# GELU times the second half, on one core: in-place GELU, packed products and three input buffers in place of two input and two output buffers

## The chip, the core and the metric

The kernel runs on one core of a Trainium2 chip. The time is device time in microseconds for one execution; before the change the median of three runs is 469.35 us (469.26 to 469.49). The core has a vector engine (VectorE, DVE in the profile), an activation engine (ScalarE, ACT), a synchronisation engine (SyncE, SP) and 16 DMA engines that move data between the chip's main memory (HBM) and the on-chip memory (SBUF), which has 128 partitions. DMA transfers are issued on a queue of SP or of ACT; an instruction waits for a semaphore to reach a count, and a finished transfer adds 16 to its semaphore.

## The reference

The input x is 32 x 512 x 2048 in float32. Each row of 2048 is cut in two halves, and the output row of 1024 is the GELU of the first half times the second half:

```python
x1, x2 = x[..., :1024], x[..., 1024:]
out = 0.5 * x1 * (1 + erf(x1 / sqrt(2))) * x2
```

That is 134.22 MB read and 67.11 MB written.

## The kernel before

The 16384 rows are cut into 16 tiles of 1024 rows. In a tile each of the 128 partitions holds R = 8 rows that lie one after the other in HBM, so that a load puts 64 KB in a row into each partition (4 rows, 32 KB, for the two halves of tile 0) and a store takes 32 KB in a row from each. There are two input buffers (x_bufs, 64 KB a partition each) and two output buffers (o_bufs, 32 KB a partition each); tile i uses number i % 2 of both.

The order on each engine is written out by hand, with one semaphore for each buffer and kind:

- SP issues the loads. Tile 0 comes in two halves, tile 1 whole; these three are issued ahead of the loop. In the loop, after tile i, SP waits until the products of tile i are done (line 108) and issues the load of tile i + 2 into the buffer that they have read (line 109). SP also issues the stores of the last two tiles.
- ACT takes each tile in pieces (5 and 3 rows; 2, 2 and 4 for the first and the last tile). Before the first piece it waits for ready[k] (line 79), which counts the load of this tile and the store that last used the same output buffer. It writes the GELU of the first half of each row into the output buffer (line 81). After the tile it waits for the products and issues the store (line 54), except for the last two tiles.
- DVE waits for each GELU piece and multiplies it, in the output buffer, with the second half of the rows in the input buffer (line 89).

Tile 0 is stored in two halves, so is tile 15; the others are stored by one transfer. At the end ACT, DVE and SP clear the semaphores, and SP waits for the last stores (line 118).

Of the kernel before, what the change touches and what calls it, by code (L numbers as in the profile page):

```python
# [1 line left out]

# [4 lines left out]

GELU = mybir.ActivationFunctionType.Gelu


@with_exitstack
def kernel(
    ctx: ExitStack,
    tc: tile.TileContext,
    x: bass.AP,
    out: bass.AP,
):
    nc = tc.nc
    P = nc.NUM_PARTITIONS

    x_flat = x.flatten_outer_dims()
    out_flat = out.flatten_outer_dims()
    n_rows, dim = x_flat.shape
    half = dim // 2

    R = 8
    x_t = x_flat.rearrange("(n p r) d -> n p r d", p=P, r=R)
    o_t = out_flat.rearrange("(n p r) d -> n p r d", p=P, r=R)
    n_tiles = x_t.shape[0]
    x_bufs = [nc.alloc_sbuf_tensor(f"x{k}_tile", [P, R, dim], x.dtype) for k in range(2)]  # L30
    o_bufs = [nc.alloc_sbuf_tensor(f"o{k}_tile", [P, R, half], out.dtype) for k in range(2)]

    first = [nc.alloc_semaphore(f"first{j}") for j in range(2)]
    ready = [nc.alloc_semaphore(f"ready{k}") for k in range(2)]
    gelu_done = nc.alloc_semaphore("gelu_done")
    mul_done = nc.alloc_semaphore("mul_done")
    tail_stored = nc.alloc_semaphore("tail_stored")
    n = {sem.name: 0 for sem in [*first, *ready, gelu_done, mul_done, tail_stored]}  # L40

    def counted(ins, sem, by):
        ins.then_inc(sem, by)
        n[sem.name] += by

    def load(i, rows, sem):
        ins = nc.sync.dma_start(out=x_bufs[i % 2][:, rows, :], in_=x_t[i][:, rows, :])  # L47
        counted(ins, sem, 16)
        return ins

    def store(queue, i, rows, sem):
        queue.wait_ge(mul_done, n[mul_done.name])
        counted(
            queue.dma_start(out=o_t[i][:, rows, :], in_=o_bufs[i % 2][:, rows, :]), sem, 16
        )

    for ins in (  # L60
        load(0, slice(0, 4), first[0]),
        load(0, slice(4, 8), first[1]),
        load(1, slice(0, 8), ready[1]),
    ):
        tc.no_tile_sem_insts.add(ins.ins.name)
    tc.close()
    tc.compile()  # L67

    for i in range(n_tiles):
        k = i % 2  # L70
        last = i == n_tiles - 1
        pieces = i == 0 or last
        steps = ((0, 2), (2, 4), (4, 8)) if pieces else ((0, 5), (5, 8))
        for lo, hi in steps:
            rows = slice(lo, hi)
            if i == 0 and lo % 4 == 0:
                nc.scalar.wait_ge(first[lo // 4], 16)
            elif lo == 0:
                nc.scalar.wait_ge(ready[k], n[ready[k].name])
            counted(  # L80
                nc.scalar.activation(  # L81
                    out=o_bufs[k][:, rows, :], in_=x_bufs[k][:, rows, :half], func=GELU
                ),
                gelu_done,
                1,
            )
            nc.vector.wait_ge(gelu_done, n[gelu_done.name])
            counted(
                nc.vector.tensor_mul(  # L89
                    out=o_bufs[k][:, rows, :],  # L90
                    in0=o_bufs[k][:, rows, :],
                    in1=x_bufs[k][:, rows, half:],
                ),
                mul_done,
                1,
            )
            if pieces and hi % 4 == 0:
                if last:
                    store(nc.sync, i, slice(hi - 4, hi), tail_stored)
                else:  # L100
                    store(nc.scalar, i, slice(hi - 4, hi), ready[k])
        if not pieces:
            if i == n_tiles - 2:
                store(nc.sync, i, slice(0, R), tail_stored)
            else:
                store(nc.scalar, i, slice(0, R), ready[k])
        if i + 2 < n_tiles:
            nc.sync.wait_ge(mul_done, n[mul_done.name])
            load(i + 2, slice(0, R), ready[k])


    nc.scalar.drain()  # L112
    for sem in (*first, *ready):
        nc.scalar.sem_clear(sem)
    nc.vector.drain()
    nc.vector.sem_clear(gelu_done)
    nc.sync.sem_clear(mul_done)
    nc.sync.wait_ge(tail_stored, n[tail_stored.name]).then_inc(
        tail_stored, -n[tail_stored.name]
    )  # L120


# [1 line left out]
_INS = ['x']  # L124
_OUTS = [((32, 512, 1024), 'float32')]


# [23 lines left out]
```

## Time and profile before

| what | before |
|---|---|
| median of three runs | 469.35 us (469.26 to 469.49) |
| span of the profiled execution | 467.9 us (its whole time is not listed; the runs' times are 1.4 to 1.6 us above it) |
| VectorE busy | 140.5 us (30%), 34 products |
| ScalarE busy | 115.5 us (25%), 34 GELUs and a table load |
| DMA queue of SP (q1) | 142.61 MB, 70.6% of the 16 engines' time |
| DMA queue of ACT (q10) | 58.72 MB, 29.1% |
| HBM traffic | 430 GB/s over the span |
| GELU, 128 x 5120 and 128 x 3072 | 4470 and 2747 ns |
| product, 128 x 5120 and 128 x 3072 | 5492 and 3351 ns |

The profile is of one execution. Its page gives the busy time of each engine, the span in 40 slices with the busy tenths of the DMA engines and the rate in GB/s, the packets of each DMA queue, the chain of work that ended last, the costliest groups of instructions with what ended the idle time before them, and the DMA issues with the median time from issue to landing. L81 stands for line 81 of the kernel; "out<-in" names what an instruction writes and reads. The chain is given in order of time as start, duration and work; "SPq" and "ACTq" are the issuing side of those engines.

### The profile page before, as it was taken

Reading aid. Unit: us, or ns where it says so; the run is one execution under the profiler, and the core shown is the slowest. Engines: PE = TensorE matmul, PEld = TensorE weight load, DVE = VectorE, ACT = ScalarE, POOL = GpSimd, SP = SyncE. Lnnn points to the kernel's source line nnn. Section 1 sums busy time; section 2 is a strip of 40 time slices with the busy share of each in tenths; the row PEclk is TensorE's granted clock in tenths of the full one; section 3 lists DMA queues with packets and bytes.
Section 4 is the critical chain, followed back from the end, with each engine's and each line's share of the span. In section 5 each row is a group of like instructions: output and inputs, shape, how many; then the busy total and the mean of one; then the engine's idle time right before and its main releaser. Section 6 shows DMA issues by size and latency. Waiting matters only on the chain.

```text
span 467.9 us, 152 instructions
## 1 busy us (share of the span) xinstructions
DVE 140.5 (30%) x34; ACT 115.5 (25%) x35; POOL 0.2 (0%) x4
## 2 busy tenths in 40 slices
DVE  0330514207052060511606116060150702507043
ACT  1320606042060410604106050050500506014060
POOL 0000000000000000000000000000000000000000
DMA  8999999999999999999999999999999999999998
GB/s 359 448 448 443 403 405 492 409 403 448 459 437 403 434 417 493 403 403 448 476 420 403 445 406 493 403 406 445 487 409 403 445 451 448 403 434 417 493 389 373
DMA packets 5041, 201.34 MB, mean 430 GB/s; under 512 B 560, under 2 KB 560, under 8 KB 560
## 3 DMA queue, kind: packets, MB, share of 16 engines
q1 hardware_dynamic: 2880, 142.61, 70.6%
q10 hardware_dynamic: 2160, 58.72, 29.1%
q14 instruction: 1, 0.01, 0.0%
HBM read 134.22 MB, written 67.11 MB: 430 GB/s over the span
## 4 chain that ended last, share of the span: by engine, by line
DMA 76%; DVE 14%; ACT 8%; ACTq 0%; SPq 0%; issue 0%
DMA out_dram<-o_tile 66%; DVE o_tile L89 14%; DMA x_tile<-in_x_dram 10%; ACT o_tile L81 8%; ACTq L112 0%; SPq L47 0%
## 5 line engine op out<-in xcount | busy, mean ns | idle before, releaser
L89 DVE TENSOR_TENSOR o_tile<-o_tile,x_tile 128x5120 f32<-128x5120 f32 (+3 forms) x34 | 140.5, 4171 | 319.7 <-ACT o_tile L81 319.7
L81 ACT ACTIVATE o_tile<-x_tile 128x5120 f32<-128x5120 f32 (+3 forms) x34 | 114.3, 3407 | 337.4 <-DMA out_dram<-o_tile 301.6
L81 ACT ACT_TABLE_LOAD x1 | 1.3, 1283 | 2.9 <-PEq L67 2.9
L135 POOL MEMSET const-bfloat16-1.0<- 128x1 bf16 x1 | 0.1, 101 | 0.0
L135 POOL MEMSET const-uint8-127<- 128x1 uint8 x1 | 0.1, 101 | 0.0
L135 POOL MEMSET const-float32-0.0<- 128x1 f32 x1 | 0.1, 98 | 0.2 <-issue 0.2
L135 POOL MEMSET const-float32-1.0<- 128x1 f32 x1 | 0.1, 98 | 0.0
## 6 DMA issues: line engine op xcount, KB each, us to landing
out_dram<-o_tile ACTq DMA_DIRECT2D x13, 4096.0 KB, 44.7
x_tile<-in_x_dram SPq DMA_DIRECT2D x2, 4096.0 KB, 16.6
out_dram<-o_tile ACTq DMA_DIRECT2D x2, 2048.0 KB, 34.5
out_dram<-o_tile SPq DMA_DIRECT2D x1, 4096.0 KB, 25.2
out_dram<-o_tile SPq DMA_DIRECT2D x2, 2048.0 KB, 7.8
x_tile<-in_x_dram SPq DMA_DIRECT2D x15, 44.2
```

What stands on the lines that cost most here:

```text
L81: nc.scalar.activation(out=o_bufs[k][:, rows, :], in_=x_bufs[k][:, rows, :half], func=GELU),
L89: nc.vector.tensor_mul(out=o_bufs[k][:, rows, :], in0=o_bufs[k][:, rows, :], in1=x_bufs[k][:, rows, half:],),
L135: nc = _bacc.Bacc("TRN2", target_bir_lowering=False, num_devices=1)
```

## The change

The output buffers go. The GELU is written over the first halves of the input rows, and the products are packed, 1024 elements each, into the front of the same buffer: row r of the output lies where half of input row r // 2 lay, which the products of the rows before have already read. There are now three input buffers (3 x 64 KB a partition, as much as 2 x 64 and 2 x 32 before), and tile i uses number i % 3. Three whole loads are issued ahead of the loop. Since a buffer also holds the products until they are stored, SP waits for the landing of the store of tile i before it issues the load of tile i + 3 into the same buffer. DVE waits for its own earlier product before each later one of a tile, because a later one writes where an earlier one has read. Tile 0 is stored by one transfer of 8 rows, not by two of 4. At the end ACT waits for all three ready counts before it clears them.

```diff
-    x_bufs = [nc.alloc_sbuf_tensor(f"x{k}_tile", [P, R, dim], x.dtype) for k in range(2)]
-    o_bufs = [nc.alloc_sbuf_tensor(f"o{k}_tile", [P, R, half], out.dtype) for k in range(2)]
+    B = 3
+    x_bufs = [nc.alloc_sbuf_tensor(f"x{k}_tile", [P, R, dim], x.dtype) for k in range(B)]
+    o_bufs = [
+        x_bufs[k][:, : R // 2, :].rearrange("p r (h d) -> p (r h) d", h=2) for k in range(B)
+    ]
...
-    ready = [nc.alloc_semaphore(f"ready{k}") for k in range(2)]
+    ready = [nc.alloc_semaphore(f"ready{k}") for k in range(B)]
...
         load(1, slice(0, 8), ready[1]),
+        load(2, slice(0, 8), ready[2]),
...
-        k = i % 2
+        k = i % B
...
-                    out=o_bufs[k][:, rows, :], in_=x_bufs[k][:, rows, :half], func=GELU
+                    out=x_bufs[k][:, rows, :half], in_=x_bufs[k][:, rows, :half], func=GELU
...
+            if lo:
+                nc.vector.wait_ge(mul_done, n[mul_done.name])
             nc.vector.wait_ge(gelu_done, n[gelu_done.name])
             counted(
                 nc.vector.tensor_mul(
                     out=o_bufs[k][:, rows, :],
-                    in0=o_bufs[k][:, rows, :],
+                    in0=x_bufs[k][:, rows, :half],
                     in1=x_bufs[k][:, rows, half:],
...
-            if pieces and hi % 4 == 0:
-                if last:
-                    store(nc.sync, i, slice(hi - 4, hi), tail_stored)
-                else:
-                    store(nc.scalar, i, slice(hi - 4, hi), ready[k])
-        if not pieces:
+            if last and hi % 4 == 0:
+                store(nc.sync, i, slice(hi - 4, hi), tail_stored)
+        if not last:
             if i == n_tiles - 2:
                 store(nc.sync, i, slice(0, R), tail_stored)
             else:
                 store(nc.scalar, i, slice(0, R), ready[k])
-        if i + 2 < n_tiles:
-            nc.sync.wait_ge(mul_done, n[mul_done.name])
-            load(i + 2, slice(0, R), ready[k])
+        if i + B < n_tiles:
+            nc.sync.wait_ge(ready[k], n[ready[k].name])
+            load(i + B, slice(0, R), ready[k])
...
     nc.scalar.drain()
+    for sem in ready:
+        nc.scalar.wait_ge(sem, n[sem.name])
```

More of the change, by code (lines that the diff above doesn't have):

```diff
@@ L46, in load @@
     def load(i, rows, sem):
-        ins = nc.sync.dma_start(out=x_bufs[i % 2][:, rows, :], in_=x_t[i][:, rows, :])
+        ins = nc.sync.dma_start(out=x_bufs[i % B][:, rows, :], in_=x_t[i][:, rows, :])
         counted(ins, sem, 16)
@@ L53, in store @@
         counted(
-            queue.dma_start(out=o_t[i][:, rows, :], in_=o_bufs[i % 2][:, rows, :]), sem, 16
+            queue.dma_start(out=o_t[i][:, rows, :], in_=o_bufs[i % B][:, rows, :]), sem, 16
         )
@@ L69 @@
     for i in range(n_tiles):
-        k = i % 2
+        k = i % B
         last = i == n_tiles - 1
-        pieces = i == 0 or last
-        steps = ((0, 2), (2, 4), (4, 8)) if pieces else ((0, 5), (5, 8))
+        steps = ((0, 2), (2, 4), (4, 8)) if i == 0 or last else ((0, 5), (5, 8))
         for lo, hi in steps:
```

## The prediction

> **What bounds the kernel now.** I read the page's head and its DMA part first, then the chain that ended last, the list of waits, and the groups by form. The DMA part, the 40 slices (first DMA share, then GB/s) and the issues:
>
> ```profile
> span 467.9 us, 152 instructions
> ...
> DMA  8999999999999999999999999999999999999998
> GB/s 359 448 448 443 403 405 492 409 403 448 459 437 403 434 417 493 403 403 448 476 420 403 445 406 493 403 406 445 487 409 403 445 451 448 403 434 417 493 389 373
> ...
> q1 hardware_dynamic: 2880, 142.61, 70.6%
> q10 hardware_dynamic: 2160, 58.72, 29.1%
> ...
> out_dram<-o_tile ACTq DMA_DIRECT2D x13, 4096.0 KB, 44.7
> ...
> x_tile<-in_x_dram SPq DMA_DIRECT2D x15, 44.2
> ```
>
> The packets of SP's queue (q1) and ACT's (q10) fill 70.6 + 29.1 = 99.7% of the time of 16 DMA engines. No slice falls under eight tenths, and only the first and last are under nine. While busy the engines move 142.61 MB in 0.706 x 467.9 = 330.3 us and 58.72 MB in 0.291 x 467.9 = 136.2 us: 431.7 and 431.3 GB/s, the same for the queue that is nearly all loads and the one that is all stores. (The GB/s of a slice swing because a packet's bytes fall into one slice; their mean is 430.) So a tile's 8.39 MB load is 19.4 us of the engines and its 4.19 MB store 9.7 us, together 29.1 us.
>
> The chain and the waits of ACT and DVE:
>
> ```profile
> 332.56 4.48 ACT o_tile L81
> 337.04 0.02 issue
> 337.06 8.77 DVE o_tile L89 x2
> 345.83 0.02 issue
> 345.86 44.68 DMA out_dram<-o_tile
> 390.54 0.02 issue
> 390.56 4.48 ACT o_tile L81
> ...
> 403.86 44.69 DMA out_dram<-o_tile
> 448.54 0.02 issue
> 448.56 1.91 ACT o_tile L81
> 450.48 1.80 ACTq L112
> 452.27 3.52 ACT o_tile L81
> 455.79 0.02 issue
> 455.81 4.42 DVE o_tile L89
> ```
>
> ```profile
> DVE o_tile L89 <- ACT o_tile L81: 319.7, 18, 21.2
> ACT o_tile L81 <- DMA out_dram<-o_tile: 301.6, 14, 21.9
> ```
>
> ACT starts every second tile 58.00 us after the last but one (332.56, 390.56, 448.56): 29.0 us a tile, which is the 29.1 us of DMA work. Compute is 4.48 + 8.77 = 13.3 us of that. The chain calls the stores the limit, and ACT's 301.6 us of waiting names them too, but a landing of 44.7 us for 9.7 us of work says only that a store stands behind the one before it and shares the engines with loads. The bound is the engines' bytes, not a buffer.
>
> **The change, part by part.** Reference: span 467.9 us, plus 469.35 - 467.9 = 1.45 us around it for the median (1.4 to 1.6 over the three runs). The sum is a difference against that span.
>
> *Bytes.* 134.22 MB read and 67.11 MB written stay. The store's source is still 32 KB in a row in each partition (four input rows of 8 KB), as with the old output buffer, so its packets keep their size. Nothing is taken from the 29.1 us a tile.
>
> *Tile 0 in one store.* Twenty transfers on q1 and fifteen on q10 give 2880 and 2160 packets, so 144 for each transfer, 16 of them the small completion ones. One transfer on ACT's queue goes: 2016 packets there, one issue of 0.36 us less on ACT (hidden: ACT is idle before L81 for 337 us). The single packet records of this trace take 0.611 us for 16 KB, 1.213 for 32 KB, 2.418 for 64 KB. Per engine, 16 of 0.611 become 8 of 1.213: 9.78 - 9.70, **-0.07 us**. The DMA page of the Trainium skill (DMA: Bandwidth & Descriptors, section "Rules for kernel authors", with the fixed-cost table of "Anatomy of one DMA") asks for few large transfers and puts a fixed cost of about 2.0 us on each; by that the sum here would be -2.0 us. The table is for the GpSimd path, which this kernel doesn't use, and a fixed cost that lies beside other packets is no engine time, so I take the packet records.
>
> The first store then goes out at 30.6 us (when the 4096-wide product of 26.11 + 4.42 ends) and not at 19.2. Cover: the loads of tiles 1 and 2, queued from the start, 38.8 us of work from 22.4 us on, so the engines have work to 61 us without any store. Without that cover it would cost up to 30.6 - 19.2 = 11.4 us.
>
> *A third load ahead.* One more issue on SP, 0.33 to 0.43 us, ahead of the barrier (L67) for which ACT waits 2.9 us before its table load. ACT then starts up to 0.4 us later, at a point where it waits until 12.76 for its first rows anyway: nothing.
>
> *The load's wait moves from the product of tile i to the landing of store i* (SP now waits for ready[k]). Behind that wait on SP stand only later loads and, at the end, the stores of tiles 14 and 15. Does the load queue run dry? Take both queues sharing in the proportion of a tile's bytes, 2 to 1, as the steady 29.0 us shows: a load lasts 29 us beside stores, 19.4 alone, and a store 29 us beside loads. Store 0 is issued at 30.6 and gets its first bytes some 2 us later (the first load's landing was 12.0 us for 9.7 us of work: 2.3 us around it). Load 1 runs alone from 22.4 to 33, then shared: lands near 46. Product 1 is done at 59.3; store 0 lands at 62, and load 3 is issued there. Load 2, begun at 46, runs until 75: **13 us of load are still queued when the new load is issued**, against 2.3 us that it needs. Store 1 follows at 62 and lands at 91, load 3 ends at 104, and so on every 29 us. The same from the buffer's side: 29 load + 13.3 compute + 29 store + two times 2.3 = 76 us, and three buffers have 87. Cost 0; if the 13 us were gone, 2.3 us a load, 13 loads, 30 us.
>
> *ACT's wait for the old store goes.* What is late next is the load: ACT will wait some 15 of 29 us for x_tile, since the DMA work of a tile is unchanged. Worth 0.
>
> *DVE's new wait on its own product.* Two products take 5.49 + 3.35 = 8.84 by their means and 8.77 in the pair, so they overlap by 0.07 us; a semaphore hop between engines is 0.02 us (51.68 to 51.70). So about 0.1 us a tile, inside 15 us of slack. In tile 15 the last product starts 0.81 us after the one before it ended (455.81 against 450.51 + 4.49), so there it costs 0.
>
> *GELU in place, product packed.* No row shows ACT writing over its own input, nor DVE writing packed over strided rows. Nearest: DVE already writes over in0 at 4.42 us for 4096. Lower end: no change (ACT's output merely gets strided as its input is; a gain would do nothing, ACT being idle three quarters of the time). Upper end: ACT falls to DVE's time per element, 5.49 against 4.47 for 5120, that is 23% on 1.91 + 1.80 + 3.52 = 7.23 us, +1.7 us. In 14 tiles the slack covers it. Only in tile 15 could it show, see the first rival. I take 0, since same-shaped instructions here differ by element count alone.
>
> *The end.* Load 15 and store 14 share SP's queue in that order, as before. When load 15 lands, all loads and stores 0 to 13 are done, as at 448.5 now (the store that ends at 448.54 was the last of them). Then the engines have store 14 (9.7 us, to 458.2) and the halves of tile 15 (4.85 each). The halves are ready 6.4 and 11.7 us after 448.5, plus 1.5 to 2.3 us from issue to first bytes: 456.4 to 457.2 against 458.2, and 461.7 to 462.5 against 463.0. So the engines don't pause, and the end is where it was. ACT's waits for ready before its clears look for stores long landed: 0.
>
> Sum: -0.07 us. Span 467.8, time 469.35 - 0.07 = **469.3 us**: no change. Between builds 0.2% (0.94 us) is about what a measurement can tell from no change.
>
> **Rivals.**
>
> *The last tile loses its cover (slower).* The second half of tile 15 has only 0.5 to 1.3 us in hand. If in-place GELU costs the 1.7 us above, the end moves by 0.4 to 1.2 us: 469.7 to 470.5. It decides from 0.5 us on; over 0.2% needs nearly the whole of it. Against: nothing in the trace slows ACT by its addresses.
>
> *The buffer cycle becomes the bound (slower).* If landings stay as they are now, a buffer needs 44.2 + 13.3 + 44.7 = 102.2 us, over three 34.1 us a tile, 5.1 us more for 13 tiles: +66 us, 535 us. With only the issue latency exposed it is the 30 us above, 499 us. For it: the issue rows and the chain read just so. Against: some 15 us of each landing is waiting behind the former transfer of the same queue, and that shrinks as fewer are queued. It decides where a store lands 13 us later than in my schedule.
>
> *Freed buffers speed it up (faster).* ACT's 301.6 us of waiting goes, and loads run a tile further ahead. But only 0.3% of the engines' time is idle: 467.9 x 0.003 = 1.4 us, so 467.9 us if all of it went. Against: the idle is start and end, which the change leaves.
>
> **How the numbers follow.** No change 0.78. Last tile 0.12, about two thirds of it beyond 0.2%: 0.08 slower, 0.04 same. Buffer cycle 0.06, all slower. Freed buffers 0.04, all faster. That would be 0.04 / 0.82 / 0.14; a change of packet times by the new order of reads and writes, which no row bounds, takes 0.04 from no change, split evenly: faster 0.06, same 0.78, slower 0.16. The range runs from 468.6 (engines' idle halved) to 470.6 (all of the last tile's case); the buffer cycle and most of the rest stay outside, under 2 in 10.
>
> **What the profile after would show.** Right: q10 with 2016 packets and the two queues still near 99.7% together; no slice under eight tenths; ACT waiting for x_tile and no longer for out_dram; SP waiting for out_dram; stores landing in 29 to 36 us instead of 44.7; products and GELUs within 2% of 5.49, 3.35 and 4.47 us; loads' landing near 42 us; tile 15's first GELU near 448.4. Wrong: a dent in the DMA row once a tile (the cycle), tile 15's last product ending over 12.2 us after its first GELU starts (the end), or packet shares summing to less or more at the same bytes.

## The result and the profile after

The changed kernel takes 470.7 us (median of five, 469.76 to 471.29) against 469.28 us before (469.09 to 469.49): 1.0027 times as long over all executions, with a 95% interval of 1.0016 to 1.0038 (the medians alone give 1.0030). The forecast was 469.3 us and no change. It is slower by 1.4 us, and its executions lie much farther apart than those of before. The profiled execution took 471.27 us, with a span of 469.6 us: 1.7 us more than the span of before.

The page of the changed kernel: its head, the two DMA rows of the 40 slices, the queues and the issues.

```profile
span 469.6 us, 171 instructions
...
DMA  8998999999999999999999999999999999999988
GB/s 357 447 441 374 469 416 438 441 438 407 441 424 444 433 416 472 441 396 433 449 430 441 424 447 435 410 447 461 391 469 416 427 452 447 407 410 455 477 373 354
DMA packets 4897, 201.34 MB, mean 429 GB/s; under 512 B 544, under 2 KB 544, under 8 KB 544
...
q1 hardware_dynamic: 2880, 142.61, 70.5%
q10 hardware_dynamic: 2016, 58.72, 29.0%
...
out_dram<-x_tile ACTq DMA_DIRECT2D x14, 4096.0 KB, 34.7
...
x_tile<-in_x_dram SPq DMA_DIRECT2D x15, 38.8
```

The reader is to see two things. First, the queues' packets took 70.5 + 29.0 = 99.5% of 469.6 us, that is 467.3 us for each engine, where before they took 99.7% of 467.9, 466.5 us: **the same bytes, in fewer packets, kept the engines busy 0.8 us longer**. The rest of the 1.7 us, 0.9 us, is engines standing idle (2.3 us for 1.4). The shares are rounded to 0.1%, half a microsecond, so this split is rough; the packet records below give it more sharply. Second, the DMA row has its dents in two places only: the fourth slice (35.2 to 47.0 us), where store 0 sets in, and the end (88 for 98 in the last two slices). Between them nothing changed, as one long window shows, first before and then after (columns: window, its length, busy time of DVE, ACT and POOL with counts, clock, DMA share, GB/s):

```profile
94.00:420.00 326.00, 96.37 (x22) 78.78 (x23) 0.00 (x0) 1.00 1.00 434
```

```profile
94.00:420.00 326.00, 97.35 (x22) 78.36 (x22) 0.00 (x0) 1.00 1.00 434
```

The waits of the changed kernel, those of ACT and DVE and then those of SP's queue:

```profile
ACT x_tile L86 <- DMA x_tile<-in_x_dram: 338.4, 17, 22.9
DVE x_tile L96 <- ACT x_tile L86: 319.5, 18, 22.9
...
SPq L52 <- DMA out_dram<-x_tile: 407.4, 13, 61.2
```

ACT no longer waits for any store, yet its waiting has grown from 337 to 338 us: it now waits as long for loads. The end of the chain, after:

```profile
414.99 35.21 DMA x_tile<-in_x_dram
450.20 0.02 issue
450.23 1.91 ACT x_tile L86
452.14 1.80 ACTq L116
453.94 3.52 ACT x_tile L86
457.45 0.03 issue
457.48 0.02 DVEq L94
457.50 0.04 issue
457.55 4.43 DVE x_tile L96
```

The last tile starts at 450.23, not 448.56, and from there it is 19.4 us to the end as against 19.3: the loss lies before the last tile. By the same chain tile 3 starts at 105.85 and tile 12 at 366.86, 29.0 us a tile as before. That points to the time before tile 3, and the packet records confirm it: from 46.5 to 450 us no packet of the changed kernel took appreciably longer than usual (0.00 us in sum for each engine).

**Where it lies.** The trace holds a record of every packet of the 16 DMA engines. Each engine carries its own sixteenth of every transfer (8 of 128 data packets), and its packets follow one another almost without a gap, so the packets can be put together into 16 chains, one for each engine. First one of 14 like engines of the changed kernel, then one of the other two, from 29 us on, then one engine of the kernel before, from 22 us on (L64 and S32 are a load packet of 64 KB and a store packet of 32 KB; start in us, duration in ns; starts are aligned on the first packet, 2.2 us):

```
14 engines  L64@29.4:2418 L64@31.8:2418 L64@34.3:3396 S32@37.6:1213 L64@38.9:2418 S32@41.3:1213
 2 engines  L64@29.7:2418 L64@32.1:3133 S32@35.2:1213 L64@36.5:4219 S32@40.7:1213 L64@41.9:2418
before      L64@22.1:2801 S16@24.9:611  L64@25.5:2444 S16@27.9:611  L64@28.5:2418 S16@31.0:611
```

Nearly everywhere else in the run a 64 KB load packet takes 2418 ns. The one just ahead of the first store packet takes 1.0 us more on 14 engines of the changed kernel, and 0.1 to 0.5 us more in the kernel before. On two engines the store gets in one load packet earlier; they lose 0.7 us there and 1.8 us at the next load packet, 2.4 to 2.5 us in all. No engine makes up for another: the one that falls behind here is still behind at the end, and the last one sets it. For what follows I add up, for each run, how much longer packets took than the usual time of their size (excess, mean over the engines, from 15 to 46.5 us), when the engines end on average, and how far the last engine ends behind that average.

### The profile page after: what moved, and what is told of

It is laid out like the page before. It is cut to its first block, busy times and chain, and to the rows that moved or that the text cites. A ratio compares the mean times of both kernels' runs of the same rounds, so it can differ in the third digit from the quotient of the medians.

```text
span 469.6 us, 171 instructions
## 1 busy us (share of the span) xinstructions
DVE 141.9 (30%) x34; ACT 115.6 (25%) x35; POOL 0.2 (0%) x4
## 3 DMA queue, kind: packets, MB, share of 16 engines
q1 hardware_dynamic: 2880, 142.61, 70.5%
q10 hardware_dynamic: 2016, 58.72, 29.0%
## 4 chain that ended last, share of the span: by engine, by line
DMA 82%; DVE 9%; ACT 6%; ACTq 0%; issue 0%; SPq 0%; DVEq 0%
DMA x_tile<-in_x_dram 46%; DMA out_dram<-x_tile 37%; DVE x_tile L96 9%; ACT x_tile L86 6%; ACTq L116 0%; SPq L52 0%; DVEq L94 0%
## 5 line engine op out<-in xcount | busy, mean ns | idle before, releaser
L96 DVE TENSOR_TENSOR x_tile<-x_tile 128x5120 f32<-128x5120 f32 (+3 forms) x34 | 141.9, 4174 | 320.1 <-ACT x_tile L86 319.5
L86 ACT ACTIVATE x_tile<-x_tile 128x5120 f32<-128x5120 f32 (+3 forms) x34 | 114.3, 3408 | 338.4 <-DMA x_tile<-in_x_dram 338.4
## 6 DMA issues: line engine op xcount, KB each, us to landing
out_dram<-x_tile ACTq DMA_DIRECT2D x14, 4096.0 KB, 34.7
x_tile<-in_x_dram SPq DMA_DIRECT2D x15, 38.8
```

What stands on the lines that cost most here:

```text
L86: nc.scalar.activation(out=x_bufs[k][:, rows, :half], in_=x_bufs[k][:, rows, :half], func=GELU),
L96: nc.vector.tensor_mul(out=o_bufs[k][:, rows, :], in0=x_bufs[k][:, rows, :half], in1=x_bufs[k][:, rows, half:],),
```

## The experiments

The expectations use letters for the theories: A, the first store costs more the later it comes; B, it costs by the size of its packets; C, the third load, the in-place buffers or the load's new wait cost by themselves; W, the first write of a run is slow as such; S, stores setting in among loads that ran alone; D, a load queue that runs dry, so that loads stop and set in anew; G, the moment at which store 0 arrives, measured against the starts of the load packets.

**First round: which part of the change.** The changed kernel with two early stores for tile 0:

```diff
+            if i == 0 and hi % 4 == 0:
+                store(nc.scalar, i, slice(hi - 4, hi), ready[k])
-        if not last:
+        if not last and i > 0:
```

> The changed kernel with one part undone: tile 0 is stored in two halves again, the first after the product of rows 2 to 4. Theory A (the loss is the first store of the run: the load packets under way when it comes are stretched, and the later it comes, among 64 KB packets of loads alone, the more): about the time of before, 469.3 us, with about 0.3 us of excess on the load packets at the first store. Theory B (the loss is the size of the first store's packets, 32 KB for 16 KB): 469.3 us too. Theory C (third load ahead, in-place buffers or the load's new wait): still 470 to 471.3 us.

Measured 469.91 us, ratio 1.0014 (1.0006 to 1.0023). More than half of the loss is gone, not all: both A and B expected 469.3.

The kernel before with only tile 0's store changed:

```diff
-            if pieces and hi % 4 == 0:
-                if last:
-                    store(nc.sync, i, slice(hi - 4, hi), tail_stored)
-                else:
-                    store(nc.scalar, i, slice(hi - 4, hi), ready[k])
-        if not pieces:
+            if last and hi % 4 == 0:
+                store(nc.sync, i, slice(hi - 4, hi), tail_stored)
+        if not last:
```

> The kernel before with that part alone: tile 0 stored by one transfer after its last product. Theories A and B: slower by about what the change cost, 470 to 471.3 us, with some load packets of 3 to 4 us near 34 us. Theory C: 469.3 us.

Measured 470.0 us, 1.0020 (1.0012 to 1.0029); 8 of its 12 executions lie at 469.48 to 470.04, four at 471.04 to 471.43. So **the single store of tile 0 makes a loss by itself**, about half of the 1.4 us in the medians, with two input buffers, separate output buffers and the old waits; C isn't needed for it. The first experiment shows that it isn't the whole: with this part undone, 0.6 us stayed. The page of a profiled execution of 469.74 us, head, rows and queues:

```profile
span 468.3 us, 151 instructions
...
DMA  8998999999999999899999899999999999989999
...
q1 hardware_dynamic: 2880, 142.61, 70.7%
q10 hardware_dynamic: 2016, 58.72, 29.0%
```

The fourth slice has the same dent, the end has none. 99.7% of 468.3 is 466.9 us, 0.4 us more than before; its packet records give 1.10 us of excess at the first store against 0.37, and the engines end 0.5 us later on average.

The changed kernel with two halves, both late:

```diff
+            if i == 0:
+                store(nc.scalar, i, slice(0, 4), ready[k])
+                store(nc.scalar, i, slice(4, 8), ready[k])
-            if i == n_tiles - 2:
+            elif i == n_tiles - 2:
```

> The changed kernel with tile 0 stored in two halves, but both issued only after its last product, near 30.6 us: 16 KB packets as before, time of the first store as after. Theory A: slow, 470 to 471.3 us. Theory B: 469.3 us. Theory C: 470 to 471.3 us.

Measured 470.05 us, 1.0021 (1.0012 to 1.0030). B, which wanted 469.3, is out as a rule for the time. The first stretch was indeed small (0.36 us near 34 us), but a second one of 0.57 us followed at 40 us.

And the small first store:

```diff
+            if i == 0 and hi == 2:
+                store(nc.scalar, i, slice(0, 2), ready[k])
         if not last:
+            if i == 0:
+                store(nc.scalar, i, slice(2, 8), ready[k])
-            if i == n_tiles - 2:
+            elif i == n_tiles - 2:
```

> The changed kernel with a small first store: rows 0 and 1 of tile 0 (8 KB a partition) go out after the first product, near 17 us, the other six rows in one transfer after the last. Theory A: the early first store takes the stretch at its cheap place, so 469.3 us or a little less, and no packets of 3 us near 34 us. Theory B: 469.3 us too, if only the first packets count; slow if 24 KB packets of the second do. Theory C: 470 to 471.3 us.

Measured 470.1 us, 1.0017 (1.0008 to 1.0026): 0.48 us of excess at the small store and 0.45 us when the second transfer's packets come. An early first store doesn't take the sting out of the next one, which goes against A too.

**Second round: is it the first write, and does the load packet's size matter?** The changed kernel itself ran beside these:

> The changed kernel as it is, once more: how its executions spread, beside the next ones on the same chip. All theories: 470 to 471.3 us, the stretched load packets near 34 us again, and the profile's DMA engines ending apart by over 1 us wherever the time is near 471.3 us.

Measured 471.48 us, 1.0031 (1.0013 to 1.0049), with two executions at 469.93 and 469.94 and five from 471.19 up. The profiled one, of 471.5 us, again has two engines that took store 0 a packet early.

An early write of zeros, with the changed kernel and with the kernel before:

```diff
+    nc.vector.memset(warm[:, :], 0.0).then_inc(warm_set, 1)
+    nc.scalar.wait_ge(warm_set, 1)
+    nc.scalar.dma_start(out=o_t[0][:, 0, 0:128], in_=warm[:, :]).then_inc(warm_out, 16)
...
                 nc.scalar.wait_ge(first[lo // 4], 16)
+                if lo == 0:
+                    nc.scalar.wait_ge(warm_out, 16)
```

> The changed kernel plus a write of 64 KB (512 B of zeros a partition) to the output by ACT's queue near 4 us, which store 0 later writes over. Theory W (the first write of a run is slow on its own, as the first read is): the stretch moves to the early packets and shrinks, no packets over 3 us near 34 us, 469.2 to 469.8 us. Theory S (what costs is that a stream of whole stores sets in among 64 KB load packets that have run alone, whatever was written before): the packets near 34 us are stretched as without it, 470 to 471.3 us.

> The kernel before plus the same early write. Theory W: the 0.3 us of excess near 22 us go, and the early write costs up to as much: 469.0 to 469.4 us. Theory S: no gain, 469.2 to 469.6 us.

Measured 471.31 us (1.0034, 1.0022 to 1.0047) and 471.06 us (1.0036, 1.0022 to 1.0049). In the changed kernel the load packets near 34 us were stretched all the same, by 0.98 us. Theory W falls. In this run ACT began 6 us late, as it waited for the write, but store 0 still went out at 30.97 us. The second run is no clean one: the write landed 14.5 us after its issue, so ACT began 6 us late and the first store went out at 25.47 us, not 19.23; it says only that the write brought nothing there either.

Tile 1 in four loads, so that store 0 meets 16 KB packets:

```diff
-        load(1, slice(0, 8), ready[1]),
+        load(1, slice(0, 2), ready[1]),
+        load(1, slice(2, 4), ready[1]),
+        load(1, slice(4, 6), ready[1]),
+        load(1, slice(6, 8), ready[1]),
```

> The changed kernel with tile 1 loaded by four transfers of two rows, so that store 0 sets in among 16 KB load packets instead of 64 KB ones. Theory S with a cost by the size of the load packets under way: the excess falls to some 0.3 us and the time to 469.5 us or so. A cost of fixed length for each engine at the first store (theory W or any other start-up): about 1 us of excess as in the changed kernel, 470 to 471.3 us.

Measured 470.43 us, 1.0023 (1.0014 to 1.0032). The excess didn't shrink with the load packets: 1.48 us, spread over about 50 packets. It isn't the length of the load packet under way that one pays.

**Third round: the rest of the first experiment.** There SP waited for store 0 longer than load 2 lasted. In this timeline of it (start, duration, work, and the idle time before it) tile 2 is in and its GELU runs before SP may issue load 3:

```profile
71.92 7.12 ACT L86 ACTIVATE x_tile<-x_tile 128x5120 f32<-128x5120 f32 x2 [17.52 <-DMA x_tile<-in_x_dram]
72.08 0.33 SPq L52 DMA_DIRECT2D x_tile<-in_x_dram  x1
```

The packet records show the engines on stores alone from 71 to 77 us, and then load packets stretched again, 0.45 us in all after 46.5 us. So, in that kernel, I gave load 3 a part that needs no store (store 0 has a semaphore of its own here, stored0):

```diff
-        if i + B < n_tiles:
+        if i == 0:
+            nc.sync.wait_ge(mul_done, n[mul_done.name])
+            load(B, slice(4, 8), ready[k])
+            nc.sync.wait_ge(stored0, n[stored0.name])
+            load(B, slice(0, 4), ready[k])
+        elif i + B < n_tiles:
```

> The changed kernel with tile 0 stored in two early halves, as in the first experiment, and load 3 cut in two: its rows 4 to 7, which the packed products don't cover, are issued after the products of tile 0, rows 0 to 3 after store 0 has landed. Theory D (in the first experiment the rest of the loss, 0.6 us, came from SP's wait for store 0, which landed at 72 us, after load 2 had ended: the load queue was dry for 5 us and the loads' new start near 77 us stretched packets again by 0.28 us): no dry load queue, 469.3 to 469.5 us. Theory C (in-place GELU, packing or the third load ahead cost by themselves): 469.9 us as there.

Measured 470.34 us, 1.0019 (1.0004 to 1.0033). The load queue is dry no more, but there are again 0.48 us of excess after 46.5 us, 0.29 of them from 68 to 72 us, where both queues pass to packets of another size at once. D alone falls: without the dry queue the loss stayed. In the two profiles the engines end 0.4 and 0.5 us later on average than before, and the excess after 46.5 us is 0.45 and 0.48 us against 0.05: what is left is again longer packets, not compute. Which part of the change brings it stays open, and theory C, whose 469.9 us lies nearer to the result than D's 469.3 to 469.5, isn't ruled out for this rest.

Four quarters, late, executed once:

```diff
+            if i == 0:
+                for lo in (0, 2, 4, 6):
+                    store(nc.scalar, i, slice(lo, lo + 2), ready[k])
-            if i == n_tiles - 2:
+            elif i == n_tiles - 2:
```

> The changed kernel with tile 0 stored in four quarters of 8 KB packets, all issued after its last product. Theory B (the stretch of the load packets just before the first store packet goes by the size of the store's packets: 0.3 us at 16 KB, 1.0 us at 32 KB): 0.1 to 0.2 us for each engine near 34 us. If the stretch goes by the time of the first store or by the bytes queued: 0.4 us or more there.

471.03 us. Near 34 us the excess is 0.14 us, as B had it, but 0.3 us follow by 44 us and 1.3 us later. With 8, 16 and 32 KB packets the first stretch among late loads was 0.14, 0.36 and 1.0 us, but 8 KB packets at 21 us paid 0.48 (the small first store above), and what is saved at the start was paid afterwards.

Two more profiles, for the engines, of the changed kernel and of the kernel before with one store:

> The changed kernel once more, for the engines. Theory G: where the time is near 471.3 us, two of the 16 engines have taken their first packet of store 0 one load packet ahead of the others and then lost over 2 us, not 1; where it is near 469.9 us, none has.

> The kernel before with tile 0 in one store, once more, for the engines. Theory G as for the changed kernel: near 471.2 us with two early engines, near 469.7 us without.

471.47 us with one engine a packet early (3302 and then 4239 ns), and 469.83 us with none.

**Fourth round: why two groups.** All 25 executions of the changed kernel together: 6 from 469.76 to 470.09, one at 470.70, 18 from 470.99 to 471.88. (Of the 92 executions of the kernel before beside all these runs, three lie at 471.79 to 472.35 and the rest under 469.8.) Store 0 is issued at 30.69 us. On most engines its first packet follows the load packet that starts at 34.1 to 34.7 us, on an early engine the one before. In the four profiles of the changed kernel the seven early engines are all ones whose earlier load packet started in the later half of the 16, at 32.13 to 32.31 us. The first load's first packet came at 2.2 us, 1.5 us after its issue began at 0.73; if store 0 takes as long, which is an estimate, it arrives near 32.2 us, just as these packets start. Some engines that started as late weren't early, so this isn't all that decides. As a test I moved the issue, and nothing else, by a GELU of 1024 elements into a spare tile (2560 in the second run):

```diff
+                if i == 0:
+                    nc.scalar.wait_ge(mul_done, n[mul_done.name])
+                    nc.scalar.activation(
+                        out=delay[:, :],
+                        in_=x_bufs[k][:, 4:8, :].rearrange("p r d -> p (r d)")[:, :1024],
+                        func=GELU,
+                    ).then_inc(delayed, 1)
+                    nc.scalar.wait_ge(delayed, 1)
                 store(nc.scalar, i, slice(0, R), ready[k])
```

> The changed kernel with store 0 issued about 1.1 us later (ACT makes a GELU of 1024 elements into a spare tile first). A 64 KB load packet lasts 2.42 us, so the store arrives in the middle of packets and not near their ends. Theory G (the slow group comes from a store that arrives near the packet ends, so that one or two engines take it a packet ahead): nearly all executions near 469.9 us, none or few over 471 us, and no engine early in the profile. If the slow group has another cause: both groups, as in the changed kernel.

> The same with a GELU of 2560 elements, about 2.4 us later: a whole load packet, so the same place against the packet ends as in the changed kernel. Theory G: both groups again, 469.9 and 471.3 us. If a later store alone is better or worse: a steady move from the run with 1.1 us.

> The changed kernel beside them: both groups, most executions near 471.3 us.

Measured on one chip: 470.16 us (1.0017, 1.0007 to 1.0028) with store 0 at 31.68 us, ten of twelve executions at 469.91 to 470.63; 471.72 us (1.0046, 1.0030 to 1.0061) with a whole packet of delay, all six at 471.46 or more; and 471.41 us (1.0036, 1.0025 to 1.0047) for the changed kernel, ten of twelve at 470.99 or more. **A store that is later by half a packet is faster, by a whole one slow again**: a trend with lateness is out, and theory G has the sign of both moves. It had expected both groups in the run with the whole packet; the lower one didn't show in its six executions, and it showed in only two of the twelve of the changed kernel beside it. The page of the run with half a packet:

```profile
span 468.8 us, 174 instructions
...
DMA  8998989999999999999999899999999999989998
...
q1 hardware_dynamic: 2880, 142.61, 70.6%
q10 hardware_dynamic: 2016, 58.72, 29.0%
```

The dent in the fourth slice is still there, the last two digits are back to 98. The engines of ten profiled executions:

| kernel | its time, us | excess 15 to 46.5 us | mean end | last engine behind the mean |
|---|---|---|---|---|
| before | not listed | 0.37 | 467.54 | 0.32 |
| before, one store | 469.74 | 1.10 | 468.07 | 0.25 |
| before, one store, again | 469.83 | 1.02 | 468.10 | 0.23 |
| changed | 471.27 | 1.18 | 468.46 | 1.24 |
| changed, again | 471.50 | 1.41 | 468.64 | 1.26 |
| changed, b | 471.47 | 1.25 | 468.69 | 1.38 |
| changed, c | 471.80 | 1.33 | 468.56 | 1.62 |
| changed, store 0 half a packet later | 470.50 | 1.35 | 468.44 | 0.32 |
| changed, store 0 a packet later | 471.77 | 1.18 | 468.80 | 1.36 |
| changed, two early stores | 470.66 | 0.40 | 467.97 | 1.22 |

From before to changed the mean end moves by 0.92 us and the last engine falls a further 0.92 us behind: together the 1.84 us between the last engines. Nine of the ten rows go by this: without an early engine 0.2 to 0.3 us, with one or two 1.2 to 1.6. The last row doesn't: there no engine was early at the first store, and why one ended late I can't say. In the profiles of the seven other runs, most of them with other first stores, the last engine ended 0.25 to 0.67 us behind. No execution of the lower group of the changed kernel as it is, at 469.8 to 470.1 us, was profiled, and none of the four upper ones of the kernel before with one store; that the lower group has no early engine and the upper one has is inferred for them from the other rows. The run with half a packet kept 1.35 us of excess: the delay took away the early engines, not the longer packets.

Not tried: a store of another shape at the very moment of the old first half with all the rest of the change kept exactly, since a later part of the tile isn't ready then. Nothing here beat the kernel before.

## Why the prediction was wrong

- *What bounds the kernel* was right: 434 GB/s in the long window both times, 29.0 us a tile, and ACT's 301.6 us of waiting for stores were worth nothing, as they became waiting for loads. That ACT would wait some 15 of 29 us was a slip: it is 29.0 - 7.1 = 21.9, since DVE's time isn't ACT's.
- *The load's new wait at 0* was right. Store 0 landed at 64.60 and load 2 was used at 76.85: 12.3 us in hand where 13 were predicted. (Both came 2 to 3 us later than in the schedule: store 0's first packets moved 4.5 to 7.4 us after its issue, not 2.) Landings were as expected (34.7 us for stores, 38.8 for loads against 42), and the buffer-cycle rival didn't come.
- *DVE's wait and the in-place GELU* were right, as the groups by form show:

```profile
L96 DVE TENSOR_TENSOR x_tile<-x_tile 128x5120 f32<-128x5120 f32 x14 | 76.9, 5492 | 283.2 <-ACT x_tile L86 283.2
L86 ACT ACTIVATE x_tile<-x_tile 128x5120 f32<-128x5120 f32 x14 | 62.6, 4470 | 306.1 <-DMA x_tile<-in_x_dram 306.1
L96 DVE TENSOR_TENSOR x_tile<-x_tile 128x3072 f32<-128x3072 f32 x14 | 47.0, 3357 | 0.5
```

  The two products take 5.50 + 3.37 with the wait, 8.88 us from start to end where 8.77 were before: 0.1 us a tile, as said. In tile 15 the last product ends 11.75 us after the first GELU starts (11.67 before), so the last-tile rival didn't come either.
- *Tile 0 in one store, -0.07 us, and its later issue hidden by loads* is **the step that failed**. The count was right (2016 packets). The cover was too: from 22 to 61 us the engines didn't lack work. But cover is only proof against idle time, and the cost came as longer packets: +0.7 us for each engine when the one store is put into the kernel before (1.10 and 1.02 against 0.37 of excess), +0.8 in the changed kernel (1.18). The trace of before had the sign of it: its own load packets at 22 us took 2.54 to 2.94 us. I had read the usual packet times and not their exceptions. By the fixed cost for each transfer that the Trainium skill states for the GpSimd path, which this kernel doesn't use (DMA: Bandwidth & Descriptors, "Anatomy of one DMA"), the one store would, as an estimate, have saved 2.0 us; measured, it cost 0.7 us (470.0 against 469.27 us).
- *The end is where it was* failed with it, because the sum treated the 16 engines as one. One or two engines that lose 2.4 to 2.7 us set the end of the whole run in the upper group of executions, 1.2 to 1.6 us behind the mean.
- The forecast named packet times in the new order as something that no row bounds and gave it 0.04, split between faster and slower. That is what came, with one of the forecast's own signs of being wrong: at the same bytes the packet shares add up to 99.5%, not 99.7%. The range ended at 470.6 us, and the median was 470.7; later runs of the same kernel gave 471.4 and 471.5.

What stays open: what in the engine or the memory makes a load packet longer when stores set in, why the sum over a start-up comes out near 0.9 to 1.5 us in most arrangements but 0.4 us in the old one, what besides the moment makes one engine early and not its neighbour, and which part of the change makes the 0.6 us that two early stores leave in the changed kernel.

## What to carry to other kernels

In a kernel whose DMA engines are full, a transfer that is moved or merged can cost time without leaving any gap: look at the durations of single packets around the place where the mix of loads and stores changes, and at the exceptions in the trace of before. Work that is split statically over engines ends with the slowest of them, so a sum of means is a lower bound. Where executions fall in two groups and an event is suspected, shift it by half the period that it may be caught in (here a load packet of 2.42 us) and by a whole one before believing in any trend.

## What the runs showed of the hardware that I had not expected

- A 64 KB load packet, 2418 ns nearly everywhere else, took 3.3 to 3.9 us on most engines when it stood just ahead of the first store packet of a whole-tile store, and up to 4.27 us on engines that were out of step. A write of 64 KB earlier in the run didn't change that (0.98 us of excess with it).
- The early write of 512 B a partition landed 14.2 and 14.5 us after its issue, though its data are 0.15 us of the engines' time at 431 GB/s; its packets took turns with the loads': each engine carried its eight, of 27 ns, one every 1.24 us, between load packets of 32 KB.
- Delaying one store by 1.0 us made the run 1.25 us faster (470.16 against 471.41 us, on the same chip), and delaying it by 2.5 us took that back (471.72 us).
